# RWKV heads 2 and 3 on the other partition half than heads 0 and 1, in a two-layer hybrid trunk

## Chip, core and metric

The kernel runs on one core of one Trainium2 chip. The metric is the device time of one execution in microseconds, as the median of several runs; lower is better.

## What is computed

Two layers of a decoder trunk on a residual stream of 1024 tokens by 1024 channels. Each layer projects the normalized stream to the inputs of four mixers (block-sparse attention, chunked spatial gating, a convolution module and RWKV-7 time mixing, 4 heads of 64 each), gates and joins them, projects back, and adds a gated embedding. The change is in RWKV alone:

```python
def step(state, inp):
    r_t, w_t, k_t, v_t, kk_t, a_t = inp
    sa = jnp.einsum('bhvk,bhk->bhv', state, -kk_t)
    state = (state * w_t[:, :, None, :]
             + sa[..., None] * (kk_t * a_t)[:, :, None, :]
             + v_t[..., None] * k_t[:, :, None, :])
    return state, jnp.einsum('bhvk,bhk->bhv', state, r_t)
...
    for i in range(DEPTH):
        h = rms_norm(x, g_pre[i]).astype(x.dtype)
        proj = h @ w_in[i]
        ...
        y_d = rwkv7_time_mix(token_shift(rw, rwkv_mu[i]), ...)
        mix = jnp.concatenate([y_a * jax.nn.silu(z_a), ..., y_d * jax.nn.silu(z_d)], axis=-1)
        x = x + rms_norm(mix @ w_out[i], g_post[i]).astype(x.dtype)
        x = x + (jax.nn.sigmoid(x @ ple_gate[i]) * (p[i] @ ple_proj[i])).astype(x.dtype)
```

## The kernel before

The program goes through two layers of two token halves (512 tokens each), four halves in all. A string of letters for each half (`ORDER`) sets the order in which the code of the mixers, the projections and the output side is written. A scheduling layer then sets the order of each engine's instructions: it takes what is ready by its own costs, first what was written first, and gives out the buffers of each pool. So dense projections stand between the small products of RWKV wherever those must wait. All dense products are split into a high and a low part and take three TensorE products each (`mm3`, lines 163 to 165, 128 rows by up to 512 columns); ScalarE and GpSimd split the weights that SyncE's DMA queue brings (lines 157, 158).

RWKV works in chunks of 64 tokens, 8 in a half. The four heads are kept in two pairs: `j` is the pair (heads 0, 1 and heads 2, 3) and `e` the head in its pair, so the head is h = 2j + e. In the channel-major inputs `AR` and `BK` of a pair, `e` is the partition half. For each chunk:

- `rwkv_ab`, through `a_block`: four products of 64 rows by 128 columns give the chunk's A matrices, in one PSUM tile for each `e` (line 438; line 441 in a 64 by 64 form for the chunks 4 to 7 in the solve). VectorE multiplies them by a mask into `AT` (line 516). `AT` has 4 buffers. Its rows and its columns both have an upper and a lower half of 64.
- `rwkv_solve` sends the triangular blocks of all chunks to DRAM (lines 452, 460), inverts them in halves on VectorE, and writes the inverses back.
- `rwkv_tri`: two groups of four 64 by 64 products (`pT`, line 533, and `pX`, line 539) with a mask on VectorE between them (line 535) and an addition behind them (line 541) join the halves of the inverse to `XF`.
- `rwkv_step`: four products of `AT` with the values (line 578) and two with the state (line 582) go to `p1`; ScalarE copies the upper half of `p1` to `Wt` (line 585); four products with `XF` give `p2` (line 589), which VectorE and ScalarE copy to `uv` (lines 591, 592); four products give the new state (line 602), and four add the chunk's output into the lower half of `p1` (line 616), which ScalarE copies to `ytok` (line 618).

Before, the four products of lines 533, 539, 578 and 616 write one and the same half of the PSUM partitions, while those of lines 589 and 602 write both halves, two products each. The PSUM tiles have tags with a number of banks each: `mm` 2, `s` 2 (attention's scores), `rp`, `pt`, `pv` and `c1` one each. Matrices of 32-bit floats are multiplied in two passes, so one product has two records in the trace, and a group of four has eight.

## Time and profile before

| | |
|---|---|
| median of 3 runs | 1924.27 us (1919.73 to 1926.44) |
| the profiled execution, first to last instruction | 2105.2 us |
| mean granted TensorE clock in it | 0.733 |
| TensorE busy | 2037.0 us (97%) |
| VectorE busy | 1350.9 us (64%) |
| ScalarE busy | 816.8 us (39%) |
| GpSimd busy | 610.7 us (29%) |

The profiled execution is a single one and longer than the timed ones; its own time is known by its span alone. Busy times of TensorE are unions of records whose ends are modelled, so two products that run side by side show as records that start almost together, and the length of a group from its first start to its last end tells more than the mean of one record.

### The profile page before, as it was taken

What the parts mean: (1) busy time and instruction counts of PE and PEld (TensorE: products, weight loads), DVE (VectorE), ACT (ScalarE), POOL (GpSimd) and SP (SyncE); (2) the same over time, 40 slices, a digit from 0 to 9 for tenths busy, and PEclk for the clock granted to TensorE, in tenths of its full rate; (3) what the DMA queues carried; (4) which work ended last, traced back from release to release, by engine and by line L of the source; (5) the groups of instructions that cost most, each with busy time, mean ns of one, the idle gap of its engine ahead of it and who ended that gap; (6) DMA issues with size and microseconds to landing.
All of it is one profiled execution on the core that took longest, in us unless ns stands there. A gap on an engine that the chain in (4) does not pass through costs nothing. (4 is left out here: it accounts for less than half of the span.)

```text
span 2105.2 us, 27656 instructions
## 1 busy us (share of the span) xinstructions
PE 2037.0 (97%) x9460; PEld 1467.7 (70%) x9460; DVE 1350.9 (64%) x3357; ACT 816.8 (39%) x1797; POOL 610.7 (29%) x487
## 2 busy tenths in 40 slices
PE   6999999999999999999999999999999999989998
PEld 4567776667776777766677766766676867767766
DVE  4347776867875745876487752767668677476362
ACT  4332234544123445544222334545322334444442
POOL 2222333112332233211233344322132323322242
PEclk7676777777776777777777777777777777767777
DMA  6434232123422322421342242431243213123343
GB/s 199 77 81 105 64 89 67 46 50 66 109 70 64 91 60 96 130 82 50 71 110 63 66 125 83 163 97 46 53 102 77 53 46 106 55 85 93 120 148 105
DMA packets 326148, 182.24 MB, mean 87 GB/s; under 512 B 88300, under 2 KB 299248, under 8 KB 326008
## 3 DMA queue, kind: packets, MB, share of 16 engines
q1 hardware_dynamic: 326008, 180.49, 31.7%
q8 instruction: 74, 1.21, 0.3%
q14 instruction: 66, 0.54, 0.1%
HBM read 149.99 MB, written 30.44 MB: 86 GB/s over the span
## 5 line engine op out<-in xcount | busy, mean ns | idle before, releaser
L158 POOL TENSOR_TENSOR wl<-ws,wh 128x512 fp32r<-128x512 f32 (+2 forms) x388 | 519.2, 1339 | 1323.9 <-ACT wh L157 1140.7
L163 PE MATMUL mm<-aT,wh 128*128 128x512 f32 (+1 forms) x1304 | 615.6, 475 | 2.9 <-ACT aT L251 2.4
L165 PE MATMUL mm<-aT,wl 128*128 128x512 f32 (+1 forms) x1304 | 617.1, 474 | 0.0
L164 PE MATMUL mm<-aT,wh 128*128 128x512 f32 (+1 forms) x1304 | 612.9, 470 | 2.1 <-DVE aT L252 1.8
L157 ACT CAST wh<-ws 128x512 fp32r<-128x512 f32 (+2 forms) x388 | 237.0, 611 | 628.2 <-PE mm L164 320.2
L164 PEld LDWEIGHTS mm<-aT,wh 128*128 128x128 f32 (+1 forms) x1304 | 269.4, 207 | 89.3 <-DVE aT L252 5.8
L163 PEld LDWEIGHTS mm<-aT,wh 128*128 128x128 f32 (+1 forms) x1304 | 266.5, 205 | 91.7 <-issue 5.9
L165 PEld LDWEIGHTS mm<-aT,wl 128*128 128x128 f32 (+1 forms) x1304 | 265.8, 204 | 85.8 <-issue 2.9
L683 DVE SCALAR_TENSOR_TENSOR cv<-cv,cw,cv 128x512 f32<-128x512 f32 x240 | 206.0, 875 | 2.4
L954 DVE TENSOR_TENSOR pt<-pt,pt 128x512 fp32r<-128x512 f32 (+1 forms) x152 | 93.8, 617 | 121.0 <-ACT pt L953 119.9
L1017 ACT ACTIVATE r<-s,sma 128x512 f32<-128x512 f32 (+3 forms) x192 | 106.1, 555 | 106.3 <-DVE sma L1015 62.2
L953 ACT CAST pt<-pt 128x512 fp32r<-128x512 f32 (+1 forms) x152 | 80.3, 528 | 134.3 <-PE pt L950 131.9
L950 PE MATMUL pt<-cst,r 128*128 128x128 f32 x528 | 113.4, 319 | 4.1 <-DVE r L1022 3.3
L950 PEld LDWEIGHTS pt<-cst,r 128*128 128x128 f32 x528 | 72.7, 150 | 30.5 <-issue 9.8
L1007 DVE CUSTOM_DVE_ANT_0 s<-s,T 128x256 f32<-128x256 f32 (+1 forms) x144 | 54.0, 375 | 58.4 <-PE s L988 57.5
L959 PE MATMUL pv<-pt,vs 128*128 128x256 f32 x264 | 87.6, 332 | 0.6 <-ACT pt L953 0.6
L960 PE MATMUL pv<-pt,vs 128*128 128x256 f32 x264 | 85.1, 334 | 1.7 <-DVE pt L954 1.4
L987 PE MATMUL s<-kv,qs 128*128 128x512 f32 (+2 forms) x192 | 79.3, 413 | 2.0 <-ACT r L1017 1.9
L988 PE MATMUL s<-kv,qs 128*128 128x512 f32 (+2 forms) x192 | 74.6, 392 | 0.0
L959 PEld LDWEIGHTS pv<-pt,vs 128*128 128x128 f32 x264 | 52.7, 200 | 28.6 <-ACT pt L953 11.3
L1022 DVE TENSOR_SCALAR r<-r,sma 128x640 f32<-128x640 f32 (+7 forms) x128 | 71.9, 562 | 0.8
L960 PEld LDWEIGHTS pv<-pt,vs 128*128 128x128 f32 x264 | 54.2, 205 | 20.1 <-DVE pt L954 7.1
(330 smaller groups left out, 3082.6 us busy)
## 6 DMA issues: line engine op xcount, KB each, us to landing
ws<-in_w_in_dram SPq DMA_DIRECT2D x232, 256.0 KB, 3.0
ws<-in_ple_gate_dram SPq DMA_DIRECT2D x64, 256.0 KB, 2.9
ws<-in_w_out_dram SPq DMA_DIRECT2D x60, 256.0 KB, 2.7
ped<-ot SPq DMA_DIRECT2D x32, 256.0 KB, 3.4
ld<-in_nsa_w_dram SPq DMA_DIRECT2D x32, 256.0 KB, 3.4
ld<-ped SPq DMA_DIRECT2D x32, 256.0 KB, 3.1
mixd<-y SPq DMA_DIRECT2D x30, 256.0 KB, 2.2
ld<-mixd SPq DMA_DIRECT2D x30, 256.0 KB, 3.2
```

What stands on the lines that cost most here:

```text
L157: nc.scalar.copy(hi[:, :cols], st[:, :cols])
L158: nc.gpsimd.tensor_sub(lo[:, :cols], st[:, :cols], hi[:, :cols].bitcast(F32))
L163: nc.tensor.matmul(out, lh, rh, start=first, stop=False, skip_group_check=shared)
L164: nc.tensor.matmul(out, lh, rl, start=False, stop=False, skip_group_check=shared)
L165: nc.tensor.matmul(out, ll, rh, start=False, stop=last, skip_group_check=shared)
L683: nc.vector.scalar_tensor_tensor(ac, xg[j][:, k:k + TH], cw[:, j * 31 + k:j * 31 + k + 1], ac, op0=OP.mult, op1=OP.add)
L950: nc.tensor.transpose(pt[:, o:o + 128], P[e][:, (b + x - b0) * 128:(b + x - b0) * 128 + 128], self.ident)
L953: nc.scalar.copy(Th[:, :n], pt[:, :n])
L954: nc.vector.tensor_sub(Tl[:, :n], pt[:, :n], Th[:, :n].bitcast(F32))
L959: nc.tensor.matmul(acc, vs, Th[:, x * 256:x * 256 + 256], start=False, stop=False)
L960: nc.tensor.matmul(acc, vs, Tl[:, x * 256:x * 256 + 256], start=False, stop=last)
L1017: nc.scalar.activation(P[:, o:o + wd], p[:, c:c + wd], AF.Exp, bias=ng[:, 0:1], accum_out=den[:, x:x + 1])
```

## The change

The places of the four heads are changed so that pair `j` has a partition half of its own. For pair 1 the two halves of `AR` change places, and with them the column halves of its A matrices. In `rwkv_tri`, `rwkv_step` and the output products, the products of pair 0 now write the upper half of the PSUM partitions and those of pair 1 the lower half (for the output `y` the other way round), and each loop goes over the heads as 0, 2, 1, 3. `XF` and `Wt` lie on 128 partitions, a half for each pair, so that `p2` reads rows 0 to 63 for pair 0 and rows 64 to 127 for pair 1. Operations of 64 partitions by 256 elements behind the products become two of 64 by 128: the mask after `pT` and the addition after `pX` on VectorE, the copy to `ytok` on ScalarE; the copy to `Wt` becomes one on ScalarE and one on VectorE. `a_blocks` writes both row halves `e` of a chunk in one loop, alternating, into two banks: `rp`, and `c1` in the solve or `s` in the steps, where before the steps used `rp` for both. The DMA of a chunk's blocks to DRAM becomes two, one for each pair.

```diff
@@ -26,7 +26,7 @@
 P_CB, P_CLG, P_CLB, P_PWB, P_GPRE, P_GPOST, P_CW, P_POS, P_N = 21, 23, 25, 27, 29, 37, 45, 107, 139
-C_ID, C_MA, C_ML, C_FAR, C_HB, C_FLAG, C_HS, C_N = 0, 128, 256, 384, 512, 640, 641, 643
+C_ID, C_MA, C_ML, C_FAR, C_HB, C_FLAG, C_HS, C_N = 0, 128, 320, 384, 512, 640, 641, 643
 S_ANTI, S_OH, S_N = 0, 128, 256
@@ -93,7 +93,7 @@
             self.SB.append(x)
-        self.nsb = self.nq = self.nb = 0
+        self.nsb = self.nq = 0
         self.onec = self.const([128, 1], "onec")
@@ -412,8 +412,8 @@
             cs = slice(4 * q, 4 * q + 4)
-            nc.vector.tensor_mul(AR[q][:, :, 0, :], c3(t1)[:, cs], c3(pr)[:, cs])
-            nc.vector.tensor_mul(AR[q][:, :, 1, :], c3(r)[:, cs], G[:, cs, 1:65])
+            nc.vector.tensor_mul(AR[q][:, :, j, :], c3(t1)[:, cs], c3(pr)[:, cs])
+            nc.vector.tensor_mul(AR[q][:, :, 1 - j, :], c3(r)[:, cs], G[:, cs, 1:65])
             nc.vector.tensor_mul(BK[q][:, :, 0, :], c3(kk)[:, cs], c3(Gi)[:, cs])
@@ -427,18 +427,18 @@
 
-    def a_block(self, q, c, e, full):
-        nc = self.nc
-        self.nb += 1
-        es = slice(64 * e, 64 * e + 64)
-        pA = self.ps("c1" if self.solving and self.nb % 2 else "rp")
-        for j in range(2):
-            bk, ar = self.BK[j][q][es, c], self.AR[j][q][es, c]
-            if full:
-                nc.tensor.matmul(pA[:, j * 128:j * 128 + 128], bk.rearrange("p a b -> p (a b)"),
-                                 ar.rearrange("p a b -> p (a b)"), start=True, stop=True)
-            else:
-                nc.tensor.matmul(pA[0:64, j * 64:j * 64 + 64], bk[:, 0], ar[:, 0], start=True, stop=True)
+    def a_blocks(self, q, c, full):
+        nc = self.nc
+        pA = [self.ps("rp"), self.ps("c1" if self.solving else "s")]
+        for j in range(2):
+            for e in range(2):
+                es = slice(64 * e, 64 * e + 64)
+                bk, ar = self.BK[j][q][es, c], self.AR[j][q][es, c]
+                if full:
+                    nc.tensor.matmul(pA[e][:, j * 128:j * 128 + 128], bk.rearrange("p a b -> p (a b)"),
+                                     ar.rearrange("p a b -> p (a b)"), start=True, stop=True)
+                else:
+                    nc.tensor.matmul(pA[e][0:64, j * 64:j * 64 + 64], bk[:, 0], ar[:, j], start=True, stop=True)
         return pA
@@ -449,13 +449,13 @@
             self.rwkv_ab(c)
-            nc.sync.dma_start(Nd[:, c * 256:c * 256 + 256].rearrange("p (h t) -> p h t", h=4),
-                              self.AT[c][0:64, :, :, 0:64].rearrange("p a b c -> p (a b) c"))
+            for j in range(2):
+                nc.sync.dma_start(Nd[:, c * 256 + j * 128:c * 256 + j * 128 + 128].rearrange("p (h t) -> p h t", h=2),
+                                  self.AT[c][0:64, j, :, 64 * j:64 * j + 64])
         ma = self.c[0:64, C_MA:C_MA + 64].unsqueeze(1).to_broadcast([64, 2, 64])
...
             Nc = self.t([128, 256], "q3", bufs=1)[:64].rearrange("p (a b c) -> p a b c", a=2, b=2)
-            for e in range(2):
-                pA = self.a_block(1, c - 4, e, False)
+            for e, pA in enumerate(self.a_blocks(1, c - 4, False)):
                 nc.vector.tensor_mul(Nc[:, :, e], pA[0:64, :128].rearrange("p (h c) -> p h c", h=2), ma)
@@ -509,10 +509,10 @@
         q, cc = divmod(c, 4)
-        ma = self.c[:, C_MA:C_MA + 128].unsqueeze(1).to_broadcast([128, 2, 128])
+        ma = self.c[:, C_MA:C_MA + 128]
+        ma = bass.AP(tensor=ma.tensor, offset=ma.offset, ap=[list(ma.ap[0]), [64, 2], [1, 128]])
         AT = self.t([128, 2, 2, 128], "at", bufs=4)
-        for e in range(2):
-            pA = self.a_block(q, cc, e, True)
+        for e, pA in enumerate(self.a_blocks(q, cc, True)):
             nc.vector.tensor_mul(AT[:, :, e], pA[:, :256].rearrange("p (h c) -> p h c", h=2), ma)
@@ -523,22 +523,25 @@
         nc = self.nc
-        fl = lambda x: x.rearrange("p a b -> p (a b)")
         hs = [slice(64 * h, 64 * h + 64) for h in range(4)]
-        N = [self.AT[c][0:64, h // 2, h % 2, 0:64] for h in range(4)]
+        pair = [slice(64 * j, 64 * j + 64) for j in range(2)]
+        cols = [slice(128 * j, 128 * j + 128) for j in range(2)]
         XY = self.t([128, 256], "x0", bufs=1)
...
         pT = self.ps("rp")
-        for h in range(4):
-            nc.tensor.matmul(pT[0:64, hs[h]], N[h], XY[0:64, hs[h]], start=True, stop=True)
+        for h in (0, 2, 1, 3):
+            j, e = divmod(h, 2)
+            nc.tensor.matmul(pT[pair[j], hs[h]], self.AT[c][0:64, j, e, pair[j]], XY[0:64, hs[h]], start=True, stop=True)
         T1 = self.t([128, 32, 8], "q4", bufs=1)[64:128].rearrange("p (a c) b -> p a (c b)", a=4)
-        nc.vector.tensor_mul(T1, pT[0:64, :256].rearrange("p (a b) -> p a b", a=4),
-                             self.c[0:64, C_ML:C_ML + 64].unsqueeze(1).to_broadcast([64, 4, 64]))
+        for j in range(2):
+            nc.vector.tensor_mul(T1[:, 2 * j:2 * j + 2], pT[pair[j], cols[j]].rearrange("p (a b) -> p a b", a=2),
+                                 self.c[pair[j], C_ML:C_ML + 64].unsqueeze(1).to_broadcast([64, 2, 64]))
         pX = self.ps("rp")
-        for h in range(4):
-            nc.tensor.matmul(pX[64:128, hs[h]], T1[:, h], XY[64:128, hs[h]], start=True, stop=True)
-        XF = self.t([64, 4, 64], "xf", bufs=4)
-        nc.vector.tensor_add(fl(XF), XY[64:128], pX[64:128, :256])
+        for h in (0, 2, 1, 3):
+            nc.tensor.matmul(pX[pair[h // 2], hs[h]], T1[:, h], XY[64:128, hs[h]], start=True, stop=True)
+        XF = self.t([128, 2, 64], "xf", bufs=4)
+        for j in range(2):
+            nc.vector.tensor_add(XF[pair[j]].rearrange("p a b -> p (a b)"), XY[64:128, cols[j]], pX[pair[j], cols[j]])
         self.XF[c] = XF
@@ -572,22 +575,23 @@
         p1, p2, p3 = pc[:, :256], pc[:, 256:384], pc[:, 384:512]
-        for h in range(4):
+        pair = [slice(64 * j, 64 * j + 64) for j in range(2)]
+        for h in (0, 2, 1, 3):
             hs = slice(h * 64, h * 64 + 64)
-            m = 64 if h else 128
-            nc.tensor.matmul(p1[:m, hs], AT[64:128, h // 2, h % 2, :m], uv[64:128, hs], start=(h == 0), stop=False,
+            j, e = divmod(h, 2)
+            nc.tensor.matmul(p1[pair[j], hs], AT[64:128, j, e, pair[j]], uv[64:128, hs], start=(e == 0), stop=False,
                              skip_group_check=True)
...
                                  self.S[:, j], start=False, stop=False, skip_group_check=True)
-        Wt = self.t([128, 256], "q1", bufs=1)[:64]
-        nc.scalar.copy(Wt, p1[0:64])
-        for h in range(4):
-            hs = slice(h * 64, h * 64 + 64)
-            es = slice(64 * (h // 2), 64 * (h // 2) + 64)
-            nc.tensor.matmul(p2[es, h % 2 * 64:h % 2 * 64 + 64], XF[:, h], Wt[:, hs], start=False, stop=True,
-                             skip_group_check=True)
+        Wt = self.t([128, 256], "q1", bufs=1)[:, :128]
+        nc.scalar.copy(Wt[0:64], p1[0:64, 0:128])
+        nc.vector.tensor_copy(Wt[64:128], p1[64:128, 128:256])
+        for h in (0, 2, 1, 3):
+            j, e = divmod(h, 2)
+            nc.tensor.matmul(p2[pair[j], e * 64:e * 64 + 64], XF[pair[j], e], Wt[pair[j], e * 64:e * 64 + 64],
+                             start=False, stop=True, skip_group_check=True)
         nc.vector.tensor_copy(uv[0:64, 0:128], p2[0:64])
@@ -610,12 +614,13 @@
             self.S = SN
-        for h in range(4):
+        for h in (0, 2, 1, 3):
             hs = slice(h * 64, h * 64 + 64)
-            n = 128 if h else 64
-            nc.tensor.matmul(p1[64:128, hs], AT[:n, h // 2, h % 2, 64:128], uv[:n, hs], start=False, stop=True,
+            j, e = divmod(h, 2)
+            nc.tensor.matmul(p1[pair[1 - j], hs], AT[:, j, e, pair[1 - j]], uv[:, hs], start=False, stop=True,
                              skip_group_check=True)
-        nc.scalar.copy(ytok[64 * (c % 2):64 * (c % 2) + 64], p1[64:128])
+        for j in range(2):
+            nc.scalar.copy(ytok[pair[c % 2], j * 128:j * 128 + 128], p1[pair[1 - j], j * 128:j * 128 + 128])
 
@@ -1254,7 +1259,7 @@
     oh[:32] = (np.arange(32)[:, None] == bucket[None, :]).astype(float) - (np.arange(32)[:, None] == 31)
-    parts = [r == c, ma, low(32), far, hb, flag, hs]
+    parts = [r == c, ma, ma[:, :64], low(32)[:, :64] | low(32)[:, 64:], far, hb, flag, hs]
     parts += [r + c == 127, oh]
...
```

The scheduling layer builds the engines' orders anew. In these rows an operation reads line, kind, out<-in and shape; `x4` is the number of equal ones in a row. A tile of tag `c1` reads as `c`, those of `l2` and `q1` as `l` and `q`.

TensorE, the first step of the first half: `p1` from `AT` (`at`) and the values (`l`), A blocks of chunk 4 (from `ab`), then `p2` from `Wt` (`q`) and `XF` (`xf`). Before:

```order
L578 MATMUL c_309_1360<-l_306_1352,at_780 128x64
L578 MATMUL c_309_1360<-l_306_1352,at_780 64x64 x3
L438 MATMUL rp_1387<-ab_447,ab_449 128x128
L438 MATMUL rp_1387<-ab_629,ab_631 128x128
L163 MATMUL mm_2018<-aT_296,wh_2021 128x512
L589 MATMUL c_309_1360<-q_310_1365,xf_1302 64x64 x4
```

After:

```order
L582 MATMUL c_309_1372<-l_306_1364,at_780 64x64 x4
L438 MATMUL rp_1401<-ab_447,ab_449 128x128
L438 MATMUL rp_1401<-ab_629,ab_631 128x128
L165 MATMUL mm_2054<-aT_291,wl_2058 128x512
L163 MATMUL mm_2054<-aT_296,wh_2057 128x512
L164 MATMUL mm_2054<-aT_297,wh_2057 128x512
L593 MATMUL c_309_1372<-q_310_1377,xf_1307 64x64 x4
```

The four products of `p1` are now one row of equal 64 by 64 products, and three dense products instead of one stand between the A block and `p2`.

TensorE, the same first half, some 200 rows ahead of that step, behind the solve's last products (`pt` is attention's compression). After, the A blocks of the row half e = 1 for the chunks 4 and 5:

```order
L860 MATMUL pt_1221<-t_230_1033,ld_1246 128x31 x4
L438 MATMUL s_1402<-ab_447,ab_449 128x128
L438 MATMUL s_1402<-ab_629,ab_631 128x128
L438 MATMUL s_1466<-ab_447,ab_449 128x128
L438 MATMUL s_1466<-ab_629,ab_631 128x128
L163 MATMUL mm_1777<-aT_281,wh_1780 128x512
```

Before, the second A block of chunk 4 stands in the second step:

```order
L578 MATMUL c_321_1416<-l_306_1352,at_795 128x64
L578 MATMUL c_321_1416<-l_306_1352,at_795 64x64 x2
L438 MATMUL rp_1391<-ab_447,ab_449 128x128
L438 MATMUL rp_1391<-ab_629,ab_631 128x128
L578 MATMUL c_321_1416<-l_306_1352,at_795 64x64
L582 MATMUL c_321_1416<-SB_77,ab_446 128x128
```

The `s` blocks of two chunks are written as soon as their inputs are there, one behind the other and both of row half e = 1, and hold the two `s` banks until the step's mask reads them; the `rp` block of the same chunk follows some 200 rows later.

VectorE, the second step of the first half (`cv` is a tap of the convolution, `q` from `rp` the mask after `pT`, `l` from `c` a half of `uv`, `SB` the state). Before:

```order
L591 COPY l_306_1352<-c_321_1416 64x128
L683 SCALAR_TENSOR_TENSOR cv_3306<-cv_1738,cw_99,cv_3306 128x512
L535 TENSOR_TENSOR q_318_1407<-rp_1402,cst 64x256
L611 SCALAR_TENSOR_TENSOR SB_79<-c_321_1416,gc_375,q_323_1431 64x64 x2
L541 TENSOR_TENSOR xf_1414<-x_316_1400,rp_1409 64x256
```

After:

```order
L653 SCALAR_TENSOR_TENSOR y_2091<-y_2091,mm_2054 128x512
L537 TENSOR_TENSOR q_318_1421<-rp_1416,cst 64x128 x2
L590 COPY q_322_1439<-c_321_1432 64x128
L688 SCALAR_TENSOR_TENSOR cv_3342<-cv_1774,cw_99,cv_3342 128x512
L544 TENSOR_TENSOR xf_1429<-x_316_1414,rp_1424 64x128 x2
L595 COPY l_306_1364<-c_321_1432 64x128
```

The copy of pair 1's half to `Wt` (line 590 of the kernel after) is new on VectorE, and mask and addition are two operations each.

## Rows read from the trace of the kernel before

**Rows 1.** The page: engine, busy (share) xinstructions; TensorE clock in 40 slices, tenths.

```profile
PE 2037.0 (97%) x9460; PEld 1467.7 (70%) x9460; DVE 1350.9 (64%) x3357; ACT 816.8 (39%) x1797; POOL 610.7 (29%) x487
...
PEclk7676777777776777777777777777777777767777
```

**Rows 2.** Waits of TensorE: line, releaser: us in all, times, longest.

```profile
PE rp L539 <- DVE q L535: 6.6, 3, 2.8
...
PE c L589 <- ACT q L585: 0.5, 1, 0.5
```

**Rows 3.** Groups by line: shapes xcount | busy us, mean ns | idle us before.

```profile
L578 PE MATMUL c<-l,at 64*64 64x64 f32 (+1 forms) x256 | 32.5, 256 | 1.2 <-ACT l L567 1.2
L539 PE MATMUL rp<-x,q 64*64 64x64 f32 x256 | 24.7, 243 | 6.6 <-DVE q L535 6.6
L533 PE MATMUL rp<-x,at 64*64 64x64 f32 x256 | 24.5, 242 | 1.8 <-DMA x<-Xd 1.7
L616 PE MATMUL c<-l,at 128*64 128x64 f32 (+1 forms) x256 | 28.0, 244 | 0.6 <-DVE SB L611 0.6
L602 PE MATMUL c<-l,bkt 128*64 128x64 f32 x240 | 17.7, 256 | 0.6 <-ACT l L592 0.6
L589 PE MATMUL c<-q,xf 64*64 64x64 f32 x256 | 17.2, 244 | 0.5 <-ACT q L585 0.5
```

**Rows 4.** Timeline of TensorE, single groups: start us, length us, line, xrecords.

```profile
237.28 0.96 PE L578 MATMUL c<-l,at 64*128 64x64 f32 x8
...
239.33 0.46 PE L589 MATMUL c<-q,xf 64*64 64x64 f32 x8
...
241.55 0.49 PE L602 MATMUL c<-l,bkt 128*64 128x64 f32 x8 [0.17 <-ACT l L592]
...
244.10 0.85 PE L616 MATMUL c<-l,at 64*64 64x64 f32 x8
...
248.85 0.45 PE L589 MATMUL c<-q,xf 64*64 64x64 f32 x4
...
259.87 0.75 PE L533 MATMUL rp<-x,at 64*64 64x64 f32 x8
...
261.44 0.75 PE L539 MATMUL rp<-x,q 64*64 64x64 f32 x8
```

**Rows 5.** Timeline of TensorE: A blocks of two row halves, then of one.

```profile
116.88 0.37 PE L438 MATMUL rp<-ab,ab 64*128 64x128 f32 x1
116.89 0.37 PE L438 MATMUL c<-ab,ab 64*128 64x128 f32 x1
...
117.39 0.32 PE L438 MATMUL c<-ab,ab 64*128 64x128 f32 x1
...
125.62 0.82 PE L438 MATMUL rp<-ab,ab 64*128 64x128 f32 x4
```

**Rows 6.** Groups by line of VectorE and ScalarE.

```profile
L683 DVE SCALAR_TENSOR_TENSOR cv<-cv,cw,cv 128x512 f32<-128x512 f32 x240 | 206.0, 875 | 2.4
L541 DVE TENSOR_TENSOR xf<-x,rp 64x256 f32<-64x256 f32 x32 | 13.5, 423 | 21.9 <-PE rp L539 21.7
L535 DVE TENSOR_TENSOR q<-rp,cst 64x256 f32<-64x256 f32 x32 | 13.4, 418 | 15.3 <-PE rp L533 14.5
...
L618 ACT COPY yt<-c 64x256 f32<-64x256 f32 x32 | 11.8, 369 | 54.6 <-PE c L616 50.5 <-DVE pt L917 3.6
L585 ACT COPY q<-c 64x256 f32<-64x256 f32 x32 | 11.7, 366 | 60.1 <-PE c L582 57.2 <-PE c L578 2.9
L591 DVE COPY l<-c 64x128 f32<-64x128 f32 x32 | 9.0, 283 | 40.3 <-PE c L589 40.2
```

**Rows 7.** Windows: busy us (xcount) of PE, PEld, DVE, ACT, POOL; clock; DMA.

```profile
626.00:646.00 20.00, 20.00 (x97) 14.19 (x97) 8.31 (x22) 2.27 (x6) 1.74 (x3) 0.53 0.13 34
242.00:262.00 20.00, 20.00 (x146) 16.04 (x144) 12.86 (x33) 5.13 (x11) 8.05 (x7) 0.75 0.24 61
```

**Rows 8.** Line 452, SyncE: xcount, ns min/median/max, first and last start.

```profile
L452 SPq DMA_DIRECT2D Nd<-at x16: 574/586/687, 118.2 to 1514.8; - x16
```

## The prediction

> **What bounds the kernel now.** I read the page first. TensorE is busy for 2037.0 us of a span of 2105.2 us, 97%, while VectorE has 64% and ScalarE 39% [rows 1]. A busy TensorE need not be TensorE at its peak, so the list of its waits comes next: none of those that belong to RWKV is long. The second product group of `rwkv_tri` waited 6.6 us for VectorE's mask, in 3 cases of 32, and `p2` waited 0.5 us once for the copy to `Wt` [rows 2]. RWKV's chain from step to step is therefore not what ends last: where it waits, dense products of lines 163 to 165 stand in between. What counts is how long each product keeps TensorE, and a microsecond taken from the small products moves everything behind it forward by about as much.
>
> The third view, groups by line, gives six kinds of groups, each of four products with two records per product. There are 32 groups of each kind (30 at line 602: 240 records of 8). They are alike in size, but not in time: the four kinds that write one PSUM half take 24.5 to 32.5 us, lines 602 and 589 take 17.7 and 17.2 us [rows 3]. The fourth view, the timeline, says why. A group of line 589 with its four products in a row lasts 0.46 us. Where that line's group was split, two products that write the same half last 0.45 us by themselves [rows 4]. So four took as long as two: the products into the upper half and those into the lower half ran side by side. The same shows for row halves: A blocks of two row halves, in two banks, run from 116.88 to 117.71, 0.83 us for eight records, and one block alone takes 0.82 us for four [rows 5].
>
> That the program need not alternate is part of this reading: line 589 is written as two products of one half and then two of the other, and still takes 0.46 us. The Trainium skill says otherwise (TensorE: Matmul & The Clock Gate, Part 3, The mechanism): products start and end in program order, without reordering. By that, line 589 would have taken twice 0.45 us less what they overlap, and the new order 0, 2, 1, 3 would give up to 32 x 0.4 = 13 us more there, which would make the time below 1875 us; the row shows that there is nothing left to give.
>
> **The change part by part.** *The four product groups.* Lines 578, 533, 539 and 616 get the pattern of lines 589 and 602: two products into each half, in a row. The order after keeps such groups whole (the first order excerpt has `p1` as one row of four). I price them twice. By all instances, with line 589 as the model for 64 rows and line 602, scaled to 32 groups (17.7 x 32/30 = 18.9 us), for the 128 rows of line 616 [rows 3]: `p1` 32.5 - 17.2 = 15.3, `pT` 24.5 - 17.2 = 7.3, `pX` 24.7 - 17.2 = 7.5, `y` 28.0 - 18.9 = 9.1, in all 39.2 us. By single undisturbed groups [rows 4]: 0.96 - 0.46 = 0.50, 0.75 - 0.46 = 0.29 twice, 0.85 - 0.49 = 0.36, together 1.44 us for a chunk and 32 x 1.44 = 46.1 us. The first has split groups in both terms, the second has none; I take the middle, 42.7 us. `p1` gains most since its first product wrote 128 columns; that form goes.
>
> *`p2`.* It already ran in two halves, so nothing is gained. It now reads rows 0 to 63 for one pair and 64 to 127 for the other, both into one bank. No row shows two row halves writing one bank. At best it stays at 0.46 us, at worst it takes the 0.75 us of line 533, 32 x 0.29 = 9.3 us [rows 4]. I take zero, because the A blocks show that two row halves run together [rows 5], and keep 9.3 us for the range.
>
> *A blocks.* Two row halves next to one another save about 0.8 us for a pair [rows 5]. But the order after shows them next to one another hardly more often than before: 7 pairs of the full form against 8, 13 of the 64 by 64 form of line 441 against 7. In the steps, where the change gives them two banks, never: the `s` blocks stand 200 rows ahead of their `rp` partners (second order excerpt). I take 1 us gained, with bounds of -0.8 (one pair less) and +2.4 (six half-size pairs at 0.4). The `s` banks are held meanwhile and attention can't have them. That costs nothing as long as dense products stand there, which they do in the order; attention starts later in the last half only.
>
> *VectorE and ScalarE.* Each 64 by 256 operation becomes two of 64 by 128, at 283 ns as at line 591: mask 32 x (2 x 283 - 418) = 4.7 us, addition 4.6 us, the new copy to `Wt` 9.1 us, 18.4 us more on VectorE [rows 6]. ScalarE loses and gains about as much as it saves: `Wt` is half as long, `ytok` two copies instead of one. Both have room [rows 1], so this counts only where a product waits for it. Three dense products cover the copy to `Wt` in the excerpt. But VectorE works in order, and a convolution tap ahead of the copy takes 875 ns [rows 6]. Bounds: nothing, or one tap in each of 32 steps, 28 us. The nearest row is TensorE's wait for the mask, 6.6 us over 32 groups [rows 2]; the copy is shorter than that mask (283 to 418 ns), so I take half, 3.3 us lost.
>
> *DMAs.* 16 more issues on SyncE at 0.58 us each [rows 8] make 9.3 us of its queue, with weight loads behind them. The weights have three buffers, and no wait of TensorE for a split weight stands in rows of the list. I take zero and keep 9.3 us.
>
> Sum: -42.7 - 1 + 3.3 = -40.4 us of 2105.2 us. The timed runs have a median of 1924.27 us, 0.914 of that span, so the gain is about 40.4 x 0.914 = 36.9 us, and the time 1924.27 - 36.9 = 1887.4, say **1887 us**.
>
> **The rivals.** *The two row halves of `p2` wait for one another.* They share a bank, and then each group takes 0.75 instead of 0.46 us. This gives back 9.3 us; with a doubled wait for VectorE (6.6) the gain is 42.7 + 1 - 9.3 - 6.6 = 27.8 us, times 0.914 25.4, so 1899 us. For it: nothing in the trace shows the opposite, and the A blocks that ran together had two banks. Against it: the two halves also write different partitions. The Trainium skill states this as a rule (TensorEngine Tiling (Array Packing), Gotcha 1): different row tiles cannot access the same PSUM bank at the same time. No row here tests it; it is the reason why this rival has a fifth of the chance.
>
> *VectorE decides.* Each chunk has three hand-offs from VectorE to TensorE (mask, addition, `Wt`), 96 in all, and each is now one operation longer or new. If two of three cost a tap of 875 ns that no dense product covers, 64 x 0.875 = 56 us are lost against 43.7 gained, 12 us slower than before: 1924 + 11 = 1935 us. It decides from 43.7/96 = 0.46 us per hand-off. For it: the one hand-off of this kind with a wait had up to 2.8 us [rows 2]. Against it: 29 of 32 of them had none.
>
> *The change doesn't do what it says:* the four groups don't run side by side, say because both products read the same 64 rows (`pT`, `pX`, `p1`). Then only waits are added: 1924 to 1930 us. Against it stands line 589, which does just that with rows 0 to 63.
>
> *The A blocks do pair in the steps,* on the chip if not in the order: 16 pairs more at 0.8 us, 12.8 us, 11.7 in timed terms, so 1876 us. Against it: 200 rows lie between them.
>
> *The clock* could move any of these. The granted clock was 0.53 of 2.4 GHz, near the 1.2 GHz level, in a stretch of 20 us in which TensorE was busy without a gap, and 0.75, between the two levels, in a stretch dense with steps [rows 7]. Steps thus don't lower it by themselves. Such a stretch costs 20 x (1 - 0.53/0.75) = 5.9 us; two more or two fewer move any time above by some 11 us.
>
> **How the numbers follow.** Forecast 58%, `p2`'s bank 18%, A blocks 8%, no effect 7%, VectorE 9%. The range runs from 1868 (46.1 + 2.4 us gained and nothing lost, 1880, less 11 for the clock) to 1910 (the bank's 1899 and 11 for the clock); outside it lie the no-effect and VectorE cases and a few per cent below. 0.3%, some 6 us, is about what a measurement of this kernel can tell from no change. Faster by more than that: 58 + 18 + 8 = 84%; within it 7%; slower 9%.
>
> **What would show it right or wrong.** In the profile after, the groups of the lines that follow 578, 533, 539 and 616 should last 0.46 to 0.49 us, with records starting in pairs, and their busy time should fall to 17 to 19 us each. The group of `p2` should stay at 0.46 us; 0.75 us would be the bank. A blocks should keep single groups of 0.82 us in the steps. TensorE's waits for the mask and for `Wt` should stay under 10 us together; 50 us there would be VectorE. TensorE's share should stay near 97%. I am wrong if the groups shrink and the span doesn't: then something other than TensorE was the bound.

## The result and the profile after

The changed kernel takes 1932.32 us (median of 8 runs, 1914.93 to 1941.12), the kernel before beside it 1921.14 us. The ratio is 1.0054, 95% interval 1.0028 to 1.0080: slower by half a per cent, where 1.9% faster was forecast, and above the forecast's range.

One thing first, without which the numbers can't be compared: the profile of before that the prediction read was of an execution at a mean granted clock of 0.733, while the timed runs of the kernel before had about 0.95 and those of the changed kernel about 0.94. The clock records of that first profile hold two values only, 0.752 and 0.5; those of every other profile here hold 1.0 and 0.5. So I took the kernel before again (label b0) and compare with that. This is the list of cores of b0, then of after (span, mean granted clock):

```profile
core 0: 1919.6 us, clock 0.952
```

```profile
core 0: 1926.5 us, clock 0.935
```

The page of b0, and behind it that of after (engine, busy, share, instructions; the clock in 40 slices):

```profile
PE 1763.1 (92%) x9460; PEld 1333.4 (69%) x9460; DVE 1378.2 (72%) x3357; ACT 810.1 (42%) x1797; POOL 619.3 (32%) x487
...
PEclk8898999899997999999999999999998999989999
```

```profile
PE 1747.8 (91%) x9460; PEld 1309.8 (68%) x9460; DVE 1399.5 (73%) x3453; ACT 810.2 (42%) x1829; POOL 620.1 (32%) x487
...
PEclk8798997899999999999999899999998989979999
```

At the clock of the timed runs TensorE had 92%, not the 97% of [rows 1], and VectorE 72%, not 64%. That is the first thing the prediction took from the wrong execution.

**The products did what was forecast.** Groups by line of after (shapes xcount | busy us, mean ns | idle us before, its releasers). Lines 582, 534, 541 and 620 are 578, 533, 539 and 616 of before; 593 and 606 are 589 and 602 [rows 3]:

```profile
L593 PE MATMUL c<-q,xf 64*64 64x64 f32 x256 | 16.0, 236 | 7.1 <-DVE q L590 7.0
L582 PE MATMUL c<-l,at 64*64 64x64 f32 x256 | 15.7, 237 | 2.9 <-ACT l L570 1.7 <-ACT yt L623 0.8
L541 PE MATMUL rp<-x,q 64*64 64x64 f32 x256 | 15.6, 243 | 12.4 <-DVE q L537 12.3
L534 PE MATMUL rp<-x,at 64*64 64x64 f32 x256 | 15.3, 242 | 13.5 <-DMA x<-Xd 13.4
L620 PE MATMUL c<-l,at 128*64 128x64 f32 x256 | 14.5, 234 | 2.9 <-DVE SB L615 2.8
L606 PE MATMUL c<-l,bkt 128*64 128x64 f32 x240 | 14.1, 240 | 3.5 <-ACT l L596 3.4
```

All six kinds now cost alike, 14.1 to 16.0 us. Single groups in the timeline of TensorE (start, length, line, xrecords), in b0 and then in after, both at a granted clock of 1.0:

```profile
238.78 0.68 PE L533 MATMUL rp<-x,at 64*64 64x64 f32 x8
...
240.17 0.68 PE L539 MATMUL rp<-x,q 64*64 64x64 f32 x8
...
243.49 0.92 PE L578 MATMUL c<-l,at 64*128 64x64 f32 x8
...
245.94 0.46 PE L589 MATMUL c<-q,xf 64*64 64x64 f32 x8
...
249.94 0.82 PE L616 MATMUL c<-l,at 64*64 64x64 f32 x8
```

```profile
236.50 0.45 PE L606 MATMUL c<-l,bkt 128*64 128x64 f32 x8
...
238.99 0.45 PE L620 MATMUL c<-l,at 128*64 128x64 f32 x8
...
241.70 0.71 PE L438 MATMUL s<-ab,ab 64*128 64x128 f32 x4
242.34 0.45 PE L534 MATMUL rp<-x,at 64*64 64x64 f32 x8
...
243.99 0.45 PE L541 MATMUL rp<-x,q 64*64 64x64 f32 x8
...
246.75 0.45 PE L582 MATMUL c<-l,at 64*64 64x64 f32 x8
247.13 0.71 PE L586 MATMUL c<-SB,ab 128*128 128x128 f32 x4
247.77 0.71 PE L438 MATMUL rp<-ab,ab 64*128 64x128 f32 x4
...
250.21 0.45 PE L593 MATMUL c<-q,xf 64*64 64x64 f32 x8 [0.59 <-DVE q L590]
```

In this stretch every group of the six lines lasts 0.45 us, where the four that changed lasted 0.68 to 0.92 us in b0 at the same clock (0.75 to 0.96 in [rows 4]). `p2` (line 593) reads two row halves and writes one bank, and still takes 0.45 us. The A blocks of the steps stand alone, 6 us apart.

**What grew are the waits.** TensorE's waits of RWKV in b0, then in after (us in all, times, longest):

```profile
PE rp L533 <- DMA x<-Xd: 12.0, 5, 4.6
...
PE rp L539 <- DVE q L535: 6.6, 8, 1.3
...
PE c L616 <- DVE SB L611: 1.5, 2, 0.8
...
PE c L589 <- ACT q L585: 0.5, 1, 0.5
```

```profile
PE rp L534 <- DMA x<-Xd: 13.4, 6, 5.4
PE rp L541 <- DVE q L537: 12.3, 13, 3.5
...
PE c L593 <- DVE q L590: 7.0, 11, 1.4
...
PE c L606 <- ACT l L596: 3.4, 4, 1.0
PE c L620 <- DVE SB L615: 2.8, 3, 1.3
```

The mask costs 12.3 us in place of 6.6, and the new copy to `Wt` 7.0 us in place of 0.5. The timeline of VectorE in after tells why, just ahead of the group at 250.21 above:

```profile
247.46 1.77 DVE L688 SCALAR_TENSOR_TENSOR cv<-cv,cw,cv 128x512 f32<-128x512 f32 x1
249.16 0.68 DVE L738 SCALAR_TENSOR_TENSOR t<-t,mm 128x512 f32<-128x512 f32 x1
249.86 0.29 DVE L590 COPY q<-c 64x128 f32<-64x128 f32 x1
```

`p1` was complete with line 586, at 247.13 + 0.71 = 247.84. The copy takes 0.29 us, but stands behind a convolution tap that here took 1.77 us and another operation. `Wt` was there 2.3 us after `p1`; an A block and dense products covered all but 0.59 us. VectorE has little idle time in such stretches. Busy time in windows (us; PE, PEld, DVE, ACT, POOL; clock; DMA), b0 and then after:

```profile
193.00:290.00 97.00, 93.19 (x699) 71.16 (x699) 81.82 (x185) 31.23 (x73) 36.05 (x30) 1.00 0.32 86
530.00:640.00 110.00, 107.13 (x722) 81.55 (x722) 81.55 (x200) 35.20 (x82) 34.48 (x31) 0.88 0.27 72
```

```profile
193.00:290.00 97.00, 87.25 (x693) 65.08 (x693) 88.67 (x202) 32.52 (x79) 37.99 (x31) 0.95 0.34 92
530.00:640.00 110.00, 100.01 (x791) 74.37 (x792) 101.01 (x244) 37.53 (x94) 39.45 (x34) 0.97 0.31 86
```

VectorE goes from 84% to 91% and from 74% to 92% there, and TensorE from 96% to 90% and from 97% to 91%. The windows lie at the same times, not at the same work: in the second, VectorE has 244 operations in after and 200 in b0, so a part of its rise is work that moved there. In two other windows (1010 to 1110 and 1450 to 1600 us) its share rises by 3 points each, and over the whole span it has 21 us more to do.

**The sum.** From all TensorE records, sorted by start, I add up the distance from each start to the next, less the wait that lies in it ("products"), and the waits apart, for the functions that the line numbers belong to; the 10 us ahead of the first product count as other waits. "Low" is the time in which the granted clock was at its lower level, 1.2 GHz. All in us; the kernels other than b0 and after are explained below. Each row is one execution; 28 timed runs of the kernel before scatter by 6.6 us (standard deviation), so a few us between two rows say little.

| kernel | span | products of step and inverse | all other products | waits in step and inverse | other waits | low |
|---|---|---|---|---|---|---|
| b0 | 1919.6 | 144.1 | 1618.8 | 24.6 | 128.0 | 183.5 |
| p1_b | 1925.0 | 145.5 | 1617.3 | 21.1 | 137.0 | 185.5 |
| p2_b | 1934.9 | 145.7 | 1632.1 | 24.0 | 128.7 | 211.8 |
| p3_b | 1932.8 | 141.6 | 1630.8 | 26.2 | 130.1 | 210.9 |
| after | 1926.5 | 103.0 | 1644.6 | 42.3 | 132.1 | 249.5 |
| p1_a | 1921.5 | 108.0 | 1636.9 | 41.0 | 131.1 | 241.0 |
| p2_a | 1914.8 | 104.7 | 1640.9 | 40.7 | 124.3 | 235.2 |
| p3_a | 1908.8 | 101.2 | 1637.4 | 36.3 | 128.9 | 226.2 |
| v6 | 1893.6 | 103.9 | 1624.1 | 27.0 | 134.4 | 191.8 |
| x1 | 1909.3 | 113.2 | 1629.0 | 27.1 | 135.9 | 186.7 |
| v3 | 1950.5 | 141.8 | 1633.9 | 29.0 | 141.7 | 225.3 |

From b0 to after: products of step and inverse -41.1 (42.7 were forecast), waits there +17.7, other waits +4.1, all other products +25.8, together +6.5; the spans differ by 6.9. The +25.8 is no added work: the program has the same 9460 products, and the time at the lower level grew by 66 us. Sorted by the level at which they started, 420 records of these products stood at the lower level in b0 and 571 in after; there they took 347 and 348 ns on the mean, at the upper level 201 ns in both. The 151 records more, at 147 ns more each, are 22 of the 25.8 us.

### The profile page after: what moved, and what is told of

Same layout as the page of the kernel before. It is cut to its first block, busy times and chain, and to the rows that moved or that the text cites. A ratio compares the mean times of both kernels' runs of the same rounds, so it can differ in the third digit from the quotient of the medians.

```text
span 1926.5 us, 27851 instructions
## 1 busy us (share of the span) xinstructions
PE 1747.8 (91%) x9460; PEld 1309.8 (68%) x9460; DVE 1399.5 (73%) x3453; ACT 810.2 (42%) x1829; POOL 620.1 (32%) x487
## 5 line engine op out<-in xcount | busy, mean ns | idle before, releaser
L158 POOL TENSOR_TENSOR wl<-ws,wh 128x512 fp32r<-128x512 f32 (+2 forms) x388 | 528.9, 1365 | 1163.0 <-ACT wh L157 1061.0
L163 PE MATMUL mm<-aT,wh 128*128 128x512 f32 (+1 forms) x1304 | 543.4, 419 | 7.1 <-DVE y L653 2.7
L164 PE MATMUL mm<-aT,wh 128*128 128x512 f32 (+1 forms) x1304 | 543.1, 417 | 3.2 <-DVE aT L252 2.9
L165 PE MATMUL mm<-aT,wl 128*128 128x512 f32 (+1 forms) x1304 | 538.5, 413 | 0.3 <-POOL wl L158 0.3
L163 PEld LDWEIGHTS mm<-aT,wh 128*128 128x128 f32 (+1 forms) x1304 | 254.4, 195 | 61.9 <-ACT aT L251 4.4
L164 PEld LDWEIGHTS mm<-aT,wh 128*128 128x128 f32 (+1 forms) x1304 | 253.9, 195 | 56.1 <-DVE aT L252 9.0
L165 PEld LDWEIGHTS mm<-aT,wl 128*128 128x128 f32 (+1 forms) x1304 | 253.7, 195 | 47.4 <-issue 1.1
L688 DVE SCALAR_TENSOR_TENSOR cv<-cv,cw,cv 128x512 f32<-128x512 f32 x240 | 217.2, 923 | 2.9
L955 PE MATMUL pt<-cst,r 128*128 128x128 f32 x528 | 98.5, 284 | 15.5 <-DVE r L1027 12.0
L955 PEld LDWEIGHTS pt<-cst,r 128*128 128x128 f32 x528 | 65.2, 144 | 44.2 <-DVE r L1027 20.8
L965 PE MATMUL pv<-pt,vs 128*128 128x256 f32 x264 | 79.5, 320 | 11.8 <-DVE pt L959 11.1
L964 PE MATMUL pv<-pt,vs 128*128 128x256 f32 x264 | 82.3, 312 | 3.1 <-ACT pt L958 3.0
L992 PEld LDWEIGHTS s<-kv,qs 128*128 128x128 f32 x192 | 39.5, 206 | 30.3 <-ACT r L1022 22.5
```

The source lines that it names most:

```text
L158: nc.gpsimd.tensor_sub(lo[:, :cols], st[:, :cols], hi[:, :cols].bitcast(F32))
L163: nc.tensor.matmul(out, lh, rh, start=first, stop=False, skip_group_check=shared)
L164: nc.tensor.matmul(out, lh, rl, start=False, stop=False, skip_group_check=shared)
L165: nc.tensor.matmul(out, ll, rh, start=False, stop=last, skip_group_check=shared)
L688: nc.vector.scalar_tensor_tensor(ac, xg[j][:, k:k + TH], cw[:, j * 31 + k:j * 31 + k + 1], ac, op0=OP.mult, op1=OP.add)
L955: nc.tensor.transpose(pt[:, o:o + 128], P[e][:, (b + x - b0) * 128:(b + x - b0) * 128 + 128], self.ident)
```

## The experiments

Ratios are against runs of the kernel before on the same chip at the same time.

### Taking the change apart

`b0`, the kernel before again: 1916.15 us, ratio 0.9986 (0.9957 to 1.0016), with TensorE at 92%.

> The kernel before once more, for a profile at the clock of the timed runs (the first one was taken at a mean granted clock of 0.733, the kernel after at 0.935). Time: 1921 us, ratio 1.00. Theory 'TensorE is no longer the only bound at the higher clock': TensorE's busy share falls from 97% to about 92%, waits of TensorE with a named releaser rise from some 60 us to over 120 us. Theory 'the saving was real but the new order costs it': the share stays at 95% or more and the waits stay under 80 us, so that the loss must be looked for in the kernel after alone.

`v1_abefore` puts the A blocks of before back into after:

```diff
-        pA = [self.ps("rp"), self.ps("c1" if self.solving else "s")]
-        for j in range(2):
-            for e in range(2):
+        for e in range(2):
+            pA = self.ps("c1" if self.solving and e == 0 else "rp")
+            for j in range(2):
...
+            yield pA
```

> The kernel after, with the A blocks written as before: row half by row half, both in bank rp in the steps (c1 and rp in the solve), so that attention's two s banks are never held. Theory 'held s banks and the new A order cost it': 1932 falls to 1915 or lower (ratio to before 0.996 or less). Theory 'VectorE's hand-offs in rwkv_tri and rwkv_step cost it': stays at 1927 to 1937 (ratio 1.003 to 1.008).

1923.19 us, 1.0032 (1.0002 to 1.0063), by its ratio at the lower end of the hand-offs theory. `v2_wact` moves the new half of `Wt` from VectorE to ScalarE:

```diff
-        nc.vector.tensor_copy(Wt[64:128], p1[64:128, 128:256])
+        nc.scalar.copy(Wt[64:128], p1[64:128, 128:256])
```

> The kernel after, with both halves of Wt copied by ScalarE. In the kernel after TensorE waited 7.0 us for VectorE's half (11 times). Theory 'hand-offs': 5 to 10 us faster than the kernel after, ratio to before 1.000 to 1.003. Theory 'held s banks': no change, ratio 1.004 to 1.007.

1919.94 us, 0.9987 (0.9961 to 1.0013), a little faster than either theory gave. `v3_bsplit` is the opposite probe: the old layout, with the new number of operations.

```diff
-        nc.vector.tensor_mul(T1, pT[0:64, :256]...
+        for j in range(2):
+            nc.vector.tensor_mul(T1[:, 2 * j:2 * j + 2], pT[0:64, 128 * j:128 * j + 128]...
...
-        nc.scalar.copy(Wt, p1[0:64])
+        nc.scalar.copy(Wt[:, 0:128], p1[0:64, 0:128])
+        nc.vector.tensor_copy(Wt[:, 128:256], p1[0:64, 128:256])
```

> The kernel before with its layout kept, but with the operations between the products split as in the change: mask and addition in two operations of 64x128 on VectorE, Wt half on ScalarE and half on VectorE, ytok in two copies. No product changes. Theory 'hand-offs': slower than before by what the change lost plus what its products saved at this clock, 15 to 40 us, ratio 1.008 to 1.02. Theory 'held s banks' or 'new A order': within 5 us of before, ratio 0.998 to 1.003.

1950.67 us, 1.0120 (1.0069 to 1.0171), as the hand-offs theory gave. But the sum doesn't show it where that theory has it. TensorE waits 29.0 us in step and inverse, only 4.4 more than in b0: more for the mask, and little for VectorE's half of `Wt`. The other products and the other waits grew by 15.1 and 13.7 us.

```profile
PE rp L540 <- DVE q L536: 11.5, 9, 3.8
...
PE c L593 <- DVE q L589: 1.7, 4, 0.8
```

`x1_bless` takes TensorE's time alone out of the kernel before. In every step but the first of a layer it leaves out the products of heads 1 to 3 at lines 578 and 616:

```diff
         for h in range(4):
+            if h and not first:
+                continue
```

> The kernel before, but in every step except the first of a layer the products of lines 578 (p1) and 616 (y) are left out for heads 1 to 3; all copies, masks and waits stay. It takes about 30 x (0.4 + 0.5) = 27 us of TensorE's own time away without any new hand-off, some two thirds of what the change saved in products (41 us between the profiles of before and after at the same clock). Theory 'TensorE's time is worth its full price, and only VectorE's new hand-offs eat it': 20 to 27 us faster, ratio 0.986 to 0.990. Theory 'what TensorE saves is given back by a lower granted clock and by waits elsewhere': 10 us faster or less, ratio 0.995 to 1.000, with a mean granted clock of 0.947 or less where before has 0.952.

1916.57 us, 0.9998 (0.9975 to 1.0021). Its page beside b0's 1763.1 us for TensorE:

```profile
PE 1742.5 (91%) x9100; PEld 1307.7 (68%) x9100; DVE 1375.5 (72%) x3357; ACT 811.0 (42%) x1797; POOL 614.8 (32%) x487
```

The products of the step fell by 32.1 us (103.6 to 71.5) and nothing came out of it in the timed runs (the profiled one in the table is the shortest of twelve). At this point the theory was: VectorE bounds the step stages as much as TensorE does, time taken from TensorE alone is worth nothing, and the added operations cost. The next three follow it and take VectorE's operations out of the new layout. `v5_wone_ab` is v1 with `Wt` as one ScalarE copy of 128x256 (two in the first step of a layer):

> The kernel after with A blocks as before (row half by row half, bank rp in the steps) and Wt copied by one ScalarE operation over 128 partitions x 256 (two in the first step of a layer). Alone, the first gave back 9 us and the second, with two ScalarE copies, 12 us. Theory 'two separate costs': 1932 - 21, 1908 to 1915, ratio 0.993 to 0.997. Theory 'one cost (the order and its clock), reached by either edit': 1917 to 1924, ratio 0.998 to 1.002.

1916.43 us, 0.9993 (0.9967 to 1.0018), in the range of the one-cost theory. `v6_tri_one` also makes mask and addition of the inverse one 128x128 operation each; for that the lower half of the inverse is loaded into the two partition halves by pair, with three DMAs for one:

```diff
-        for j in range(2):
-            nc.vector.tensor_mul(T1[:, 2 * j:2 * j + 2], pT[pair[j], cols[j]]...
+        nc.vector.tensor_mul(T1.rearrange("p (a b) -> p a b", a=2), pT[:, :128]...
...
-        for j in range(2):
-            nc.vector.tensor_add(XF[pair[j]].rearrange("p a b -> p (a b)"), XY[64:128, cols[j]], pX[pair[j], cols[j]])
+        nc.vector.tensor_add(XF.rearrange("p a b -> p (a b)"), XY[:, 0:128], pX[:, 0:128])
```

> As the kernel before this one, and rwkv_tri's hand-offs in one operation each: the lower part of the inverse is loaded so that each pair has its own partition half (three DMAs for one), so that mask and addition are one operation of 128x128 on VectorE each (283 ns, where before had 418 and 423 and the change 2 x 283). Products side by side as in the change. Theory 'hand-offs': TensorE's wait for the mask falls from 12.3 us to 7 or less, and the time to 1890 to 1905, ratio 0.985 to 0.993. Theory 'clock and waits elsewhere give it back': 1910 to 1920, ratio 0.995 to 1.000. The two DMAs more per chunk may cost: wait for x over 20 us would show it.

1891.73 us, 0.9865 (0.9832 to 0.9898): faster than both kernels. Its waits and its page:

```profile
PE rp L543 <- DVE q L538: 9.5, 8, 2.2
...
PE c L597 <- ACT q L594: 0.9, 2, 0.5
```

```profile
PE 1728.3 (91%) x9460; PEld 1297.2 (69%) x9460; DVE 1365.6 (72%) x3357; ACT 814.4 (43%) x1831; POOL 618.2 (33%) x487
```

The wait for `Wt` is gone (0.9 us), and the mask waits 8 times as in b0, not 13. In the table above its products stay short (103.9), the waits of step and inverse fall back to 27.0, and so does the time at the lower clock, 191.8. `v7_tri_one_s` is v6 with the change's own A blocks:

> The same, but with the change's own A blocks (alternating row halves, banks rp and s in the steps). Theory 'held s banks cost': 6 to 12 us slower than the one with A blocks as before. Theory 'they cost nothing, the order alone moved': within 4 us of it.

1905.36 us, 0.9936 (0.9910 to 0.9963), 14 us slower than v6 where 6 to 12 were expected of the held banks.

### VectorE's load by itself

The theory says that VectorE's load counts. `y1_vload` adds some; `y2_btaps` takes some out, by leaving out three of the thirty taps of the convolution; `y3_ataps` and `y4_blesstaps` have the edit of y2 in after and in x1.

```diff
+        jk = self.t([128, 8], "jk", bufs=1)
+        for j in range(2):
+            nc.vector.reduce_max(jk[0:64, j:j + 1], uv[0:64], axis=AX.X)
```

> The kernel before, with two reductions (reduce_max of 64x256) added on VectorE behind every step of the loop over chunks; nothing waits for their results. By the reductions of the same width in the trace (0.42 us) the 64 of them are some 27 us of VectorE in the step stages, and TensorE's own work is unchanged. Theory 'VectorE's load': VectorE is as much a bound there as TensorE, so 10 to 25 us come out, 1926 to 1941. Rival 'hand-offs': what costs is only the time from one product's end to the next one's start through VectorE, and idle load costs little: within 5 us of the kernel before.

1948.49 us, 1.0175 (1.0127 to 1.0222). The 64 reductions took 24.5 us on VectorE, and the kernel became 29 us longer by the medians: more than their whole time, and above the range of either theory.

```diff
-            for k in range(1, 31):
+            for k in range(1, 28):
```

> The kernel before with the 15-, 31-tap convolution's VectorE loop cut by three taps of thirty (the output is not the reference's): 24 taps of 0.91 us, 22 us less VectorE in the stages where the RWKV steps run; TensorE's work is unchanged. Theory 'VectorE's load': 12 to 20 us faster, 1896 to 1905. Rival 'hand-offs': 0 to 5 us.

1955.17 us, 1.0178 (1.0142 to 1.0215): slower, with a tenth of the taps gone. VectorE's row of the taps in y2 (240 of them took 214.1 us in b0) and two of TensorE's waits (11.3 and 6.6 us in b0):

```profile
L683 DVE SCALAR_TENSOR_TENSOR cv<-cv,cw,cv 128x512 f32<-128x512 f32 x216 | 194.5, 916 | 2.7
```

```profile
PE pt L950 <- DVE r L1022: 16.9, 22, 2.1
...
PE rp L539 <- DVE q L535: 10.6, 10, 3.2
```

VectorE has 20 us less to do and TensorE waits longer for it. No theory of load or of hand-offs forecast this. Both expectations fell.

> The changed kernel with the same three taps left out (the output is not the reference's). Theory 'VectorE's load': with 22 us of VectorE gone, the 18 us that the change adds there are more than made up, TensorE's 41 us of shorter product groups come out in part, and it is faster than the kernel before with the same taps out: 1880 to 1895, 10 us or more below that. Rival 'hand-offs': it stays as far above the kernel before with the taps out as the changed kernel stands above the kernel before, 5 to 11 us.

1922.78 us, 1.0027 (1.0001 to 1.0053): 32 us below y2, but not at the 1880 to 1895 of the load theory.

> The kernel before with both left out: the products of heads 1 to 3 for p1 and y in every step but the first of a layer (27 us of TensorE by its trace) and three of the thirty taps (22 us of VectorE); the output is not the reference's. Alone the products gave nothing (ratio 0.9998). Theory 'VectorE's load' (two bounds side by side): together they give more than the taps alone, 5 to 20 us more, 1880 to 1895. Rival 'TensorE's length in the steps is hidden for another reason (hand-offs, clock)': no faster than the taps alone, within 4 us.

1902.43 us, 0.9913 (0.9880 to 0.9946): 53 us below y2, where 5 to 20 were expected. So with the taps out the change is worth 1.0027/1.0178 = 0.985, and the products left out in x1 are worth 0.974, where without the tap edit they gave 1.0054 and 0.9998. The same edit has another sign or size on another neighbour. What else differs is the order: the scheduling layer builds it anew for each kernel. In the traces, 16% of TensorE's records stand elsewhere in y2 than in before, and about a third in after.

### The order by itself

So I moved the order and left the work nearly as it was. One copy of a single column (64x1, read by nobody) is added in 32 places, the same in both kernels: `p1` by VectorE behind each step, `p2` by VectorE behind each inverse, `p3` by ScalarE behind each step. The 32 copies took 4.4 us on VectorE in p1_b, 4.7 us in p2_b and 6.1 us on ScalarE in p3_b; no run separates what they cost by themselves from what the new order costs.

```diff
+        nc.vector.tensor_copy(self.t([128, 8], "jk", bufs=1)[0:64, 0:1], uv[0:64, 0:1])
```

> The kernel before with one copy of a single column (64x1) by VectorE behind every step, whose result nobody reads: 32 copies, some 2 to 3 us of VectorE. The work is otherwise the same, but the scheduling layer puts 1581 of TensorE's 8038 instructions elsewhere. Theory 'order': the time moves by the order alone, 8 to 40 us to either side of the kernel before. Rival 'VectorE's hand-offs explain the result': the time stays within 6 us of the kernel before.

> The changed kernel with the same one-column copy behind every step (1883 of TensorE's instructions stand elsewhere than in the changed kernel). Theory 'order': 8 to 40 us to either side of the changed kernel, and over the three pairs of such copies the changed layout comes out 10 to 30 us below the old one on the mean. Rival 'hand-offs': within 6 us of the changed kernel, 5 to 15 us above the kernel before with the same copies.

> The kernel before with the one-column copy by VectorE behind the triangular inverse's last addition, 32 in all (2016 of TensorE's instructions stand elsewhere). Theory 'order': 8 to 40 us to either side of the kernel before. Rival 'hand-offs': within 6 us of it, at most 3 us slower for the copy.

> The changed kernel with that copy at the same place (2549 of TensorE's instructions stand elsewhere). Theory 'order': 8 to 40 us to either side of the changed kernel, on the mean of the pairs below the old layout. Rival 'hand-offs': within 6 us of the changed kernel and 5 to 15 us above the kernel before with the same copy.

> The kernel before with the one-column copy behind every step by ScalarE in place of VectorE, 32 in all (1526 of TensorE's instructions stand elsewhere). Theory 'order': 8 to 40 us to either side of the kernel before. Rival 'hand-offs': within 6 us of it.

> The changed kernel with ScalarE's one-column copy behind every step (1243 of TensorE's instructions stand elsewhere). Theory 'order': 8 to 40 us to either side of the changed kernel, on the mean of the pairs below the old layout. Rival 'hand-offs': within 6 us of the changed kernel and 5 to 15 us above the kernel before with the same copy.

Ratios, all against the kernel before as it is:

| copy | old layout | new layout | new over old |
|---|---|---|---|
| none | 1 | 1.0054 (1.0028 to 1.0080) | +0.5% |
| p1 | 1.0035 (1.0003 to 1.0066) | 1.0045 (1.0024 to 1.0066) | +0.1% |
| p2 | 1.0091 (1.0062 to 1.0119) | 0.9970 (0.9945 to 0.9994) | -1.2% |
| p3 | 1.0091 (1.0061 to 1.0122) | 0.9960 (0.9936 to 0.9984) | -1.3% |

Adding a copy that nobody reads moves the old layout by up to 0.9%, 17 us, and the new one by 0.9% the other way. p1 hardly moves either: there the expected 8 us are missed. The rival (each stays within 6 us, the new layout stays above) fell in p2 and p3. The order of before is the fastest of the four old ones, that of after the slowest of the four new ones. On the mean the new layout is 1.0007 to the old one's 1.0054, 0.5% faster; the four differences scatter by 0.9% (standard deviation), so the 95% interval of their mean takes in zero, and the sign of the layout's own worth stays open. A gain of 1.9% can't be read from them.

What does not scatter is the table of sums. Waits of p3_b, then of p3_a:

```profile
PE rp L539 <- DVE q L535: 10.8, 8, 3.9
```

```profile
PE rp L541 <- DVE q L537: 12.4, 12, 3.5
...
PE c L593 <- DVE q L590: 5.4, 9, 1.4
```

Over the four orders the products of step and inverse fall from 144.2 to 104.2 us (-40.0), the waits there rise from 24.0 to 40.1 (+16.1), all other products rise from 1624.8 to 1640.0 (+15.2) as the time at the lower clock rises from 198 to 238 us, and other waits fall by 1.8. That leaves -10.5 us, and the mean spans differ by 10.2. The ranges of old and new don't overlap, in these waits (21.1 to 26.2 against 36.3 to 42.3) or in the time at the lower clock (184 to 212 against 226 to 250); v6, with the operations taken out again, lies by the old ones in both (27.0 and 192 us). So do the waits of x1, which has less TensorE time in the steps and no new hand-off, and of v3, which has the new hand-offs and the old products (27.1 and 29.0 us). So neither brought the waits by itself, each tried in one order; the 36 to 42 us came with both, shorter products and more operations between them.

The luck of the old order shows in the same table. Against b0, p2_b and p3_b have 28 and 27 us more at the lower clock and 13 and 12 us more in the other products, while their waits in step and inverse differ from b0's by less than 2 us.

## Why the prediction was wrong, step by step

**Right: the four product groups.** 42.7 us forecast, 41.1 measured from b0 to after and 40.0 over four orders; 0.45 us a group, as line 589 was read. The new order alternates the halves and line 589 of b0 does not, and their groups are equally short: the program need not alternate, as [rows 4] had shown.

**Right: `p2`.** Zero was taken, and the group stayed at 0.45 us with two row halves writing one bank. Had they waited for one another it would have taken what line 533 takes in b0, 0.68 us; the rival that carried 18% fell. The Trainium skill (TensorEngine Tiling (Array Packing), Gotcha 1) states that different row tiles cannot access the same PSUM bank at the same time; the trace disagrees here, with 0.45 us.

**Right: A blocks and DMAs.** A blocks stayed single in the steps. The DMA wait of the inverse went from 12.0 to 13.4 us, in the new orders 8.1 to 13.4. What the `s` banks cost stays open: v1 against after and v6 against v7 both favour the old A blocks (0.2% and 0.7%), but such differences lie within what an order does.

**Wrong: "a microsecond taken from the small products moves everything behind it forward by about as much".** This is the step that failed: it gave the products their full price and put almost nothing on the other side. It rested on 97% [rows 1], read in an execution at a clock of 0.733. There the products of line 163 had a mean of 475 ns, 416 ns in b0, and by the same sums TensorE waited 64 us; in b0 it waits 152.6 us. From b0 to after 41.1 us of products went, and 21.8 us of waits and 25.8 us of slower other products came. What such a microsecond is worth alone stays open: x1 took 32.1 us out and gave 0.9998, but with the taps out the same edit gave 0.974, more than its full price.

**Wrong in size: VectorE.** 3.3 us was taken, 17.7 measured from b0 to after and 16.1 over four orders. The bounds (0 to 28) held it; the row chosen for it was the wrong one. The 6.6 us of [rows 2] were three waits in the profile at 0.733; at the clock of the runs there were eight before the change and 13 after, and no row had a copy to `Wt` on VectorE, for which TensorE then waited 7.0 us. "Both have room" was an average over the span; in the step stages VectorE has 84% and 74% in b0. Removing the operations again (v6) removed the waits; adding them without the shorter products (v3) brought only 4.4 us. The term came from a row in which the products were still long.

**Missing: the clock as a consequence.** The prediction had it as a chance of 11 us to either side, and zero in the sum. Its reading of [rows 7], that 0.75 in a stretch of steps lay between the two levels, was wrong: 0.752 was the upper of the two values in that execution, so the row could not show what steps do to the clock at the timed runs. The new layout has more time at the lower level in all four orders, and the other products pay 15.2 us. Over the 19 kernels profiled here at this clock, the time at the lower level goes with the waits in step and inverse (correlation 0.83; 0.97 among the ten with the new layout, 0.52 among the nine with the old). x1, whose products are shorter without new hand-offs, has 187 us, v6 192 us. That the waits cause it is a reading, not shown, and not the whole of it: p2_b and p3_b have more time at the lower level without more of these waits, and no run changed the clock alone.

**Missing: the order.** No rival was about it, and the sign of the result changes with it. About 10 us of the result are that the order of before is the best of four (1 against a mean of 1.0054), some 9 us that the order of after is the worst of four (1.0054 against 1.0007). That before had a good order and after a bad one is luck, and nothing in the prediction bears on it. The scaling by 0.914 is small beside this: 3.5 us.

Together, with 1921 us for 100%: -40.0 + 16.1 + 15.2 - 1.8 = -10.5 us for the layout, + 10 + 9 for the two orders, some +9 us against the measured +11. The two order terms are differences from the means of the same ratios, so this sum has to come out; what it tells is the size of the parts. The rival "VectorE decides" gave 1935 us, near the result, by 56 us of waits that aren't there; the number was close, and its mechanism had less than a third of the size.

The criterion at the end was the right one: the groups shrank, the span didn't, so TensorE's time was not all that counted.

## What to carry to other kernels

Compare the granted clock of the profiled execution with that of the timed runs before a share of busy time is taken for the bound, and read the shares in the stages that change. When a layout splits an operation on the engine that the bounding engine waits for, count each new hand-off at what stands ahead of it in that engine's queue, and rebuild until the number of operations is what it was: v6 did so on VectorE and reached 0.9865, in the one order that it was run in. Where a scheduler rebuilds the order at every edit, run a few neutral edits on both sides first; a difference smaller than their scatter (0.9% here) is no verdict on the idea.

## What was not expected of the hardware

- Two row halves that write different partitions of one bank ran side by side: line 593, eight records in 0.45 us, as quick as line 589 of b0 with one row half (0.46 us).
- Time follows the mean granted clock closely from run to run of the same program: over 28 runs of the kernel before, 0.945 to 0.959, a hundredth of clock goes with 15 us (correlation -0.92; 12 to 14 us in four other sets of such runs).
- 32 added copies of one column moved the time by up to 17 us, with 4 to 6 us of work of their own; 24 convolution taps less made it 34 us longer. That the rebuilt order does it is the reading that is left, and no run changed the order with the work exactly the same.
